# A two-layer decoder step: state-space tables begun at half step four, sums of a Strassen-like product's weights moved, residual loaded in quarters

## The chip, the cores and the metric

The kernel runs on one core of a Trainium2 chip. A core has five engines with a queue each: TensorE for matrix products (PE; its weight loads are listed as PEld), VectorE (DVE), ScalarE (ACT), GpSimd (POOL) and SyncE (SP), which here issues nearly all DMA transfers. The engines work on a shared on-chip memory and wait for each other through semaphores; each takes its own instructions strictly in order. The metric is the time of one execution in microseconds of device time, and the runs are compared by their median. TensorE's clock is granted by the chip at one of two levels, 2.4 GHz (1.00 in the profile's rows) or 1.2 GHz (0.50).

## The reference, cut to what matters

One step of a decoder trunk with two layers, a Conformer convolution layer and a diagonal state-space layer, each followed by a dense SwiGLU network and residual adds. Here 1024 prompt tokens and 64 sample tokens are treated together as 1088 columns; the width is 1024 and the hidden width 2816, in float32.

```python
def swiglu(h, w_gate, w_up, w_down):
    return (jax.nn.silu(h @ w_gate) * (h @ w_up)) @ w_down

for i in range(DEPTH):            # layer 0: convolution, layer 1: state space
    ...
    yp = yp + dp
    yp = yp + swiglu(rms_norm(yp, norm_ffn[i]), w_gate[i], w_up[i], w_down[i])
y_prompt = rms_norm(yp, norm_final)
```

The state-space layer needs tables that depend on its parameters alone (input, output and in-chunk kernel matrices of 64 groups), not on the tokens.

## The kernel before

A float32 product is made of three products of rounded parts: each operand is split into a high part (an ACT copy with rounding) and a low part (a DVE subtraction), and high x high, high x low and low x high are accumulated. `operand` does such a split (L592 on ACT, L593 on DVE), `halfprod` (L600) the matrix products. On top of that the products of the dense network go by a scheme of seven products instead of eight: weights, tokens and outputs are cut into 2 x 2 quarters ("11", "12", "21", "22"), some products take sums or differences of quarters, and the results are added into the outputs' quarters.

The up projection, `ffn_up`, walks over 11 pairs of hidden blocks (`q`), each with a half step for the gate and one for the up weights; a half step is seven products of 24 matmuls. In layer 0, `extra` is called at the end of each half step from the second pair on, with the running number 2q or 2q+1. There it is `tables`, which from number `TU` on begins one of 16 pieces of the state-space tables (`ssm_tables`) per half step and finishes the piece begun the half step before: loads by SP, products on POOL and DVE (L487 to L492, L504 to L506), a copy on ACT (L510), four products on PE into `kr` (L515), eight steps of a sum on DVE (L527, L529), and three stores into DRAM (L476: `st_v`, `st_w`, `st_tt`). Their scratch tiles `b` are in a pool `tab`, eight buffers of one tag.

The down projection, `ffn_down`, works through the products in the order 1, 6, 5, 3, 7, 4, 2, each over 11 hidden pairs `p` and four output blocks `j`. Its token operands were stored by `ffn_up` in DRAM (`td`) and are loaded into `f0b` or `f1b` (L876), its weights into `f0a`, `f1a` (L844), and split into `da` and `db`. Product 6 needs sums of weight quarters, two POOL operations per pair (L856, L857), product 3 one (L863). After a product `collect` (L899) adds the accumulated banks into the residual `xr`, which is loaded as eight whole blocks of 128 x 1088 when the first product is done (L938). The split tokens `db` have three buffers in the pool `bg`. In layer 0 `bg` is opened when the pools `tab` and `mix` of the up projection are closed, at the same address.

The raw weights, tokens and residual blocks share 35 large buffers with the up projection's operands. A scheduler orders each engine's queue by simulating it from the program's order; so the place of an instruction in a queue is not the place in the code.

Of the kernel before, what the change touches and what calls it, by code (L numbers as in the profile page):

```python
# [34 lines left out]
GF = P // C  # L35
GU = GF // 2
NU = G // GU
TU = 5
NLV = 7
EPS = 1e-6  # L40
TB = 68
# [1 line left out]
HT, QT = NT // 2, NT // 4  # L43
NPR, NKP = NFF // 2, NFB // 2
# [18 lines left out]
def decoder_kernel(ctx: ExitStack, tc: tile.TileContext, A):  # L63
    nc = tc.nc
    V, S, PE, GP, SP = nc.vector, nc.scalar, nc.tensor, nc.gpsimd, nc.sync
# [14 lines left out]
    def big(name, dt=F32):  # L80
        return bpool.tile([P, NT], dt, tag="big", name=name)
# [41 lines left out]
    def load_weight(src, name, behind=None):  # L123
        return split_weight(*fetch_weight(src, name), behind)
# [151 lines left out]
    summed = sums.mm  # L276
# [318 lines left out]
    def halfprod(ps, a, ac, an, b, first, last, subs=(0, 1), at=0, more=False):  # L595

        for i, (ah, bh) in enumerate(((0, 0), (0, 1), (1, 0))):
            for s in subs:
                bo = bh * HT + s * QT
                mm = PE.matmul(  # L600
                    ps[s - at][:, :QT],
                    a[:, ah * an + ac : ah * an + ac + P],
                    b[:, bo : bo + QT],
                    start=first and i == 0,
                    stop=last and i == 2,
                    skip_group_check=more,
                )
        return mm

    xd = [[dram.tile([P, NT], F32, name=f"xd{i}_{fb}") for fb in range(NFB)] for i in range(2)]  # L610
# [219 lines left out]

    def ffn_down(layer, name, on_chunk, on_block, before_last, ws, bg, bs):
        order = (1, 6, 5, 3, 7, 4, 2)
        into = {1: "11", 6: "21", 5: "22", 3: "12", 7: "22", 4: "21", 2: "11"}
        NJ = NFB // 2
        kept = {}

        def raw(w, p, use):

            pp = p // 2
            if (w, pp, use) not in kept:  # L840
                t = kept[w, pp, use] = big(f"{name}a{w}_{pp}_{use}")
                m = min(2, NPR - 2 * pp)
                k = ("11", "22", "21", "12").index(w)
                SP.dma_start(  # L844
                    t[:, : m * 512].rearrange("p (t c) -> p t c", t=m),
                    A["down"][layer, k, 2 * pp : 2 * pp + m].rearrange("t p c -> p t c"),
                )
            return kept[w, pp, use][:, (p % 2) * 512 : (p % 2 + 1) * 512]

        def weights(i, p):  # L850

            if i == 1:
                return raw("11", p, 0)
            if i == 6:
                s1, s2 = raw("22", p, 0), raw("21", p, 0)
                GP.tensor_add(s1, s2, s1)  # L856
                GP.tensor_sub(s2, s1, raw("11", p, 0))  # L857
                return s2
            if i == 5:
                return raw("22", p, 0)  # L860
            if i == 3:
                s4 = raw("12", p, 0)
                GP.tensor_sub(s4, s4, raw("21", p, 0))  # L863
                return s4
            if i == 7:
                s3 = raw("21", p, 1)
                GP.tensor_sub(s3, raw("11", p, 1), s3)  # L867
                return s3
            return raw("22" if i == 4 else "12", p, 1)
# [9 lines left out]
        def operands(i, p):  # L879
            last = i == order[-1]  # L880
            if last and p > 2:
                ga = big(f"{name}da{i}_{p}", F32R)
            else:
                ga = wpool.tile([P, D], F32R, tag="wg", name=f"{name}da{i}_{p}", bufs=6)
            if last and p < NPR - 3:
                gb = big(f"{name}db{i}_{p}", F32R)
            else:
                gb = bg.tile([P, NT], F32R, tag="bg", name=f"{name}db{i}_{p}", bufs=3)
            operand(ga, 512, weights(i, p))
            operand(gb, HT, tokens(i, p))  # L890
            return ga, gb

        def quarter(j, w):
            o = (int(w[1]) - 1) * HT
            return xr[2 * j + int(w[0]) - 1][:, o : o + HT]

        def collect(i, j, bank, s):
            c = quarter(j, into[i])[:, s * QT : (s + 1) * QT]
            V.tensor_add(c, c, bank[:, :QT])  # L899
# [6 lines left out]
        def done(j, w, o=None, n=HT):  # L906

            fb = 2 * j + int(w[0]) - 1
            o = (int(w[1]) - 1) * HT if o is None else o
            if on_block is not None:  # L910
                on_block(fb, o, n)
            return fb, o

        xr, early, begun = [], [], {}
        for i in order[:-1]:
            if TAKES[i] is None:
                ps = []
                for j in range(NJ):
                    bank = mm_bank if j < 3 else aux_bank
                    ps.append([bank(f"{name}d{i}_{j}_{s}") for s in range(2)])  # L920
            groups = [(0, 1)] + [(p,) for p in range(2, NPR - 2)] + [(NPR - 2, NPR - 1)]
            for g in groups:
                ops = begun.pop(i) if i in begun else [operands(i, p) for p in g]
                for j in range(NJ):
                    for p, (ga, gb) in zip(g, ops):
                        halfprod(ps[j], ga, j * P, 512, gb, TAKES[i] is None and p == 0, p == NPR - 1, more=TAKES[i] is not None)
                if i == order[-2] and g[0] >= 3:
                    early.append(operands(order[-1], len(early)))
                if i == order[-2] and g[0] == 2:
                    for j in range(NJ):  # L930
                        ss.add(xr[2 * j + 1], 2 * j + 1, HT, HT)
            k = order[order.index(i) + 1]
            if k != order[-1]:
                begun[k] = [operands(k, p) for p in groups[0]]
            if not xr:
                for fb in range(NFB):
                    xr.append(big(f"{name}xr{fb}"))
                    SP.dma_start(xr[fb], xd[layer][fb])  # L938
                xt[:] = xr
            for j in range(NJ):  # L940
                for s in range(2):
                    collect(i, j, ps[j][s], s)
                if i == 4:
                    done(j, "21")
                if i == 7:
                    done(j, "22")
                if i == 3:
                    fb, o = done(j, "12")
                    ss.add(xr[fb], fb, o, HT)
# [6 lines left out]
        i = order[-1]  # L956
# [29 lines left out]
        def end(j, s):  # L986
            collect(i, j, bank[j], s)
            ss.piece = lambda nm: squares[s][:, j * QT : (j + 1) * QT]
            fb, o = done(j, "11", s * QT, QT)
            ss.add(xr[fb], fb, o, QT)  # L990
# [346 lines left out]
    with ExitStack() as st:  # L1337
# [4 lines left out]
        for ci in range(len(CH)):  # L1342
# [11 lines left out]
            for fb in range(ahead):  # L1354
                o, n = CH[ci]
# [4 lines left out]
        for fb in range(ahead, NFB):  # L1360
            t = xt[fb]
            w = load_weight(A["pw2"][fb], f"pw2_{fb}")
# [9 lines left out]
        def tables(f, after):  # L1372

            with tc.issue_after(after.ins), tc.issue_after(loaded.ins):
                for g in begun:
                    next(g, None)
                begun.clear()
                if TU <= f < NU + TU:
                    g = ssm_tables(tab, f - TU)
                    next(g)  # L1380
# [41 lines left out]
    with layer0:  # L1422
        bg, bs = [layer0.enter_context(tc.tile_pool(name=nm, bufs=2)) for nm in ("bg0", "bs0")]
        ffn_down(0, "f0", step_scales, store_x, lambda: [load_stash(fb) for fb in range(2)], ws, bg, bs)
# [251 lines left out]
    with layer1:  # L1676
        bg, fin = [layer1.enter_context(tc.tile_pool(name=nm, bufs=2)) for nm in ("bg1", "bs1")]
        ffn_down(1, "f1", finish, None, None, ws, bg, fin)
# [145 lines left out]
```

## Time and profile before

| | us |
|---|---|
| median of 3 runs | 2283.67 |
| lowest and highest | 2278.57, 2284.53 |
| the profiled execution | 2288.31 |
| its span, first to last instruction | 2286.5 |
| TensorE busy | 2151.0 |
| VectorE busy | 1669.1 |
| GpSimd busy | 1082.2 |

Layer 0's up projection ends and its down projection begins between 954 and 994 us of the span, layer 1's between 2003 and 2024. A timeline row has the start, the duration (of several merged instructions their whole stretch, if there is an xcount), engine, line, operation, output <- inputs, shapes, and in brackets how long the engine was idle before it and what ended that. Rows of SPq are issues of DMA transfers; when the data lands is told by the landing rows.

### The profile page before, as it was taken

Reading aid. Unit: us, or ns where it says so; the run is one execution under the profiler, and the core shown is the slowest. Engines: PE = TensorE matmul, PEld = TensorE weight load, DVE = VectorE, ACT = ScalarE, POOL = GpSimd, SP = SyncE. Lnnn points to the kernel's source line nnn. Section 1 sums busy time; section 2 is a strip of 40 time slices with the busy share of each in tenths; the row PEclk is TensorE's granted clock in tenths of the full one; section 3 lists DMA queues with packets and bytes.
Section 4 is the critical chain, followed back from the end, with each engine's and each line's share of the span. In section 5 each row is a group of like instructions: output and inputs, shape, how many; then the busy total and the mean of one; then the engine's idle time right before and its main releaser. Section 6 shows DMA issues by size and latency. Waiting matters only on the chain. (4 is left out here: it accounts for less than half of the span.)

```text
span 2286.5 us, 39847 instructions
## 1 busy us (share of the span) xinstructions
PE 2151.0 (94%) x15760; PEld 2114.0 (92%) x15760; DVE 1669.1 (73%) x2458; ACT 828.7 (36%) x1618; POOL 1082.2 (47%) x1000
## 2 busy tenths in 40 slices
PE   8998878989999999979998889998999999999997
PEld 7998877989999999979998889998999999998997
DVE  7975867697799999968575973339766666669486
ACT  4201126253333333323453442225333333333363
POOL 3368854465476677635132230116453453428033
PEclk9999988999999999989999999998999999999998
DMA  5489374313244544494295663211322322377532
GB/s 213 158 235 307 127 246 183 131 57 123 92 173 148 189 173 171 158 383 170 94 334 197 232 231 104 92 63 38 124 90 79 117 91 95 121 279 278 186 125 79
DMA packets 198427, 370.73 MB, mean 162 GB/s; under 512 B 15968, under 2 KB 90848, under 8 KB 198240
## 3 DMA queue, kind: packets, MB, share of 16 engines
q1 hardware_dynamic: 173024, 355.34, 44.5%
q10 hardware_dynamic: 25216, 12.85, 2.1%
q8 instruction: 123, 2.02, 0.3%
q14 instruction: 64, 0.52, 0.1%
HBM read 259.34 MB, written 108.79 MB: 161 GB/s over the span
## 5 line engine op out<-in xcount | busy, mean ns | idle before, releaser
L600 PE MATMUL f0d<-f0db,f0da 128*128 128x272 f32 x1848 | 237.0, 290 | 17.5 <-ACT f0db L592 15.6
L600 PEld LDWEIGHTS f0d<-f0db,f0da 128*128 128x128 f32 x1848 | 234.3, 189 | 19.5 <-ACT f0db L592 15.8
L600 PE MATMUL f1d<-f1db,f1da 128*128 128x272 f32 x1848 | 240.7, 292 | 5.3 <-DVE f1da L593 2.2
L600 PEld LDWEIGHTS f1d<-f1db,f1da 128*128 128x128 f32 x1848 | 237.4, 191 | 7.7 <-DVE f1da L593 3.6
L593 DVE TENSOR_TENSOR f0db<-f0b,f0db 128x544 fp32r<-128x544 f32 x77 | 72.7, 950 | 51.7 <-ACT f0db L592 51.6
L593 DVE TENSOR_TENSOR f1db<-f1b,f1db 128x544 fp32r<-128x544 f32 x77 | 74.9, 981 | 45.0 <-ACT f1db L592 44.9
L1095 PE MATMUL dw<-u,tz 128*128 128x128 f32 x640 | 82.2, 291 | 17.8 <-DMA tz<-in_toep 16.6
L1095 PEld LDWEIGHTS dw<-u,tz 128*128 128x128 f32 x640 | 80.0, 206 | 19.3 <-DMA tz<-in_toep 15.4
L592 ACT ACTIVATE f0db<-f0b 128x544 fp32r<-128x544 f32 x77 | 49.9, 656 | 112.8 <-PE f0d L600 91.9
L592 ACT ACTIVATE f1db<-f1b 128x544 fp32r<-128x544 f32 x77 | 50.0, 655 | 98.9 <-PE f1d L600 96.5
L593 DVE TENSOR_TENSOR f0da<-f0a,f0da 128x512 fp32r<-128x512 f32 x77 | 73.0, 954 | 11.9 <-ACT f0da L592 11.6
L593 DVE TENSOR_TENSOR f1da<-f1a,f1da 128x512 fp32r<-128x512 f32 x77 | 75.0, 987 | 6.8 <-ACT f1da L592 6.8
L235 POOL TENSOR_TENSOR f1acc<-f1acc,f1t 128x544 f32<-128x544 f32 x10 | 13.4, 1361 | 111.1 <-ACT f1t L234 111.1
L1634 DVE SCALAR_TENSOR_TENSOR gs<-gv,cst,gs 128x408 f32<-128x408 f32 (+1 forms) x24 | 12.8, 590 | 68.9 <-PE gv L131 68.2
L235 POOL TENSOR_TENSOR f0nacc<-f0nacc,f0nsq 128x544 f32<-128x544 f32 (+1 forms) x13 | 15.5, 1208 | 98.8 <-issue 60.6
L235 POOL TENSOR_TENSOR f1nacc<-f1nacc,f1nsq 128x544 f32<-128x544 f32 (+1 forms) x13 | 16.6, 1284 | 93.6 <-ACT f1nsq L234 93.4
L782 ACT ACTIVATE f0t<-f0t 128x544 f32<-128x544 f32 x44 | 29.1, 661 | 82.0 <-DVE f0t L781 62.8
L782 ACT ACTIVATE f1t<-f1t 128x544 f32<-128x544 f32 x44 | 29.1, 661 | 78.2 <-DVE f1t L781 52.6
L529 DVE SCALAR_TENSOR_TENSOR b<-kr,cst,b 128x448 f32<-128x448 f32 (+6 forms) x112 | 54.5, 487 | 1.2
L592 ACT ACTIVATE f0da<-f0a 128x512 fp32r<-128x512 f32 x77 | 47.2, 620 | 20.4 <-DMA f0a<-in_down 11.0
L592 ACT ACTIVATE f1da<-f1a 128x512 fp32r<-128x512 f32 x77 | 46.9, 622 | 16.2 <-POOL f1a L867 7.3
L491 POOL TENSOR_TENSOR b<-b,b 128x512 f32<-128x512 f32 x32 | 50.5, 1598 | 1.2
(3087 smaller groups left out, 6505.6 us busy)
## 6 DMA issues: line engine op xcount, KB each, us to landing
f0b<-td SPq DMA_DIRECT2D x77, 272.0 KB, 6.7
f1b<-td SPq DMA_DIRECT2D x77, 272.0 KB, 5.3
tz<-in_toep SPq DMA_DIRECT2D x32, 640.0 KB, 6.8
f0a<-in_down SPq DMA_DIRECT2D x40, 512.0 KB, 7.2
f1a<-in_down SPq DMA_DIRECT2D x40, 512.0 KB, 5.7
td<-f0t SPq DMA_DIRECT2D x22, 544.0 KB, 5.8
td<-f1t SPq DMA_DIRECT2D x22, 544.0 KB, 5.2
f0gate<-in_gate SPq DMA_DIRECT2D x22, 512.0 KB, 4.4
```

The source lines that it names most:

```text
L235: self.last = E.tensor_add(acc, acc, t[:, :n])
L491: GP.tensor_mul(v, v, b.unsqueeze(2).to_broadcast([P, GU, 2, PS]))
L529: V.scalar_tensor_tensor(tv[:, :, s:], kv[:, :, : L - s], col(K_MJ, s), tv[:, :, s:], op0=ALU.mult, op1=ALU.add)
L592: S.activation(out[:, :n], x, AF.Copy)
L593: EL.tensor_sub(out[:, n : 2 * n], x, out[:, :n].bitcast(F32))
L600: mm = PE.matmul(ps[s - at][:, :QT], a[:, ah * an + ac : ah * an + ac + P], b[:, bo : bo + QT], start=first and i == 0, stop=last and i == ...
L782: S.activation(c[w], c[w], AF.Silu)
L1095: ln["dw"] = PE.matmul(ps[:, g * P : (g + 1) * P], tz[:, (g % 2) * NM + m].rearrange("p c i -> p (c i)"), uv[:, h * GU + g, PADC - m : PAD ...
L1634: V.scalar_tensor_tensor(sg[:, o : o + n], p[:, :n], col(K_BGV, fb), sg[:, o : o + n], op0=ALU.add, op1=ALU.mult)
```

## The change

Three edits. The tables begin at half step 4 instead of 5. Under product 1 of a down projection, from pair 3 to pair 8, the weight sums of product 6 are made for pairs 0 to 5 (`AHEAD = 3`); a set `summed` keeps them from being made twice. And `fetch` loads quarters of the residual, four of 128 x 544 before the first collect that adds into them, in place of eight whole blocks.

```diff
-TU = 5
+TU = 4
...
     def ffn_down(layer, name, on_chunk, on_block, before_last, ws, bg, bs):
         order = (1, 6, 5, 3, 7, 4, 2)
+        AHEAD = 3
...
-        kept = {}
+        kept, summed = {}, set()
...
             if i == 6:
                 s1, s2 = raw("22", p, 0), raw("21", p, 0)
-                GP.tensor_add(s1, s2, s1)
-                GP.tensor_sub(s2, s1, raw("11", p, 0))
+                if p not in summed:
+                    summed.add(p)
+                    GP.tensor_add(s1, s2, s1)
+                    GP.tensor_sub(s2, s1, raw("11", p, 0))
                 return s2
...
+        here = set()
+
+        def fetch(j, w):
+
+            here.add(w)
+            o = (int(w[1]) - 1) * HT
+            SP.dma_start(quarter(j, w), xd[layer][2 * j + int(w[0]) - 1][:, o : o + HT])
+
...
+                if i == 1 and AHEAD <= g[0] < NPR - 2:
+                    weights(6, g[0] - AHEAD)
...
             if not xr:
                 for fb in range(NFB):
                     xr.append(big(f"{name}xr{fb}"))
-                    SP.dma_start(xr[fb], xd[layer][fb])
                 xt[:] = xr
+            if into[i] not in here:
+                for j in range(NJ):
+                    fetch(j, into[i])
```

What this makes of the queues is seen at two places. The first is the end of layer 0's up projection. On SP, the queue before: `td0_10` are the stores of the last hidden pair, `st_tt7<-b15_8` is the last store of the last table, `f0a` and `f0b` are weights and tokens of the down projection (`f0b1_5` the last tokens of product 1).

```order
L876 DMA f0b1_4_10424<-td0_9_238 128x544
L844 DMA f0a11_5_0_10461<-in_down 128x512
L825 DMA td0_10_239<-f0t10_1_9607 128x1088
L824 DMA td0_10_239<-f0t10_0_9606 128x1088
L827 DMA td0_10_239<-f0u10_9608 128x1088
L829 DMA td0_10_239<-f0t38_9880 128x544
L476 DMA st_tt7_684<-b15_8_10115 128x512
L876 DMA f0b1_5_10465<-td0_10_239 128x544
```

The last table's store stood behind the stores of the last half step; now it stands ahead of the first load of the down projection:

```order
L476 DMA st_w17_676<-b15_7_9880 128x512
L476 DMA st_v17_668<-b15_1_9619 128x512
L476 DMA st_tt7_684<-b14_8_9609 128x512
L1417 DMA ld_w13_12577<-st_w13_672 128x1024
L476 DMA st_tt7_684<-b15_8_9891 128x512
L845 DMA f0a11_0_0_10160<-in_down 128x2x512
L879 DMA f0b1_0_10164<-td0_0_229 128x544
```

It has moved by one half step, in front of the loads and of the stores `td0_10`. On PE at the same place, before, the products `kr15` of the last table stand among those of the last half step `f0up10`:

```order
L600 MATMUL f0up10m1_0_9889<-f0b5_3_4569,f0up10a5_9951 128x272
L600 MATMUL f0up10m1_1_9890<-f0b5_3_4569,f0up10a5_9951 128x272
L515 MATMUL kr15_10107<-b15_5_9875,b15_4_9873 128x128 x3
L600 MATMUL f0up10m7_0_9988<-f0b4_0_4663,f0up10a4_10043 128x272 x2
L600 MATMUL f0up10m7_1_9989<-f0b4_0_4663,f0up10a4_10043 128x272 x2
```

and now between the last two half steps, all four together:

```order
L600 MATMUL f0gate10m1_0_9657<-f0b3_3_4686,f0gate10a3_9848 128x272
L600 MATMUL f0gate10m1_1_9658<-f0b3_3_4686,f0gate10a3_9848 128x272
L515 MATMUL kr15_9883<-b15_5_9634,b15_4_9632 128x128 x4
L600 MATMUL f0up10m1_0_9910<-f0b1_0_3720,f0up10a1_9907 128x272
L600 MATMUL f0up10m1_1_9911<-f0b1_0_3720,f0up10a1_9907 128x272
```

`f0up10` has no table product inside any more.

The second place is the start of layer 1's down projection. On POOL before, the subtraction `f1t38`, which feeds the last store of the last half step, stands ahead of all sums of product 6 (`f1a22`, `f1a21`):

```order
L783 TENSOR_TENSOR f1t10_0_20275<-f1t10_0_20275,f1r_15597 128x544
L828 TENSOR_TENSOR f1t38_20508<-f1t10_1_20276,f1u10_20277 128x544
L856 TENSOR_TENSOR f1a22_0_0_21117<-f1a21_0_0_21119,f1a22_0_0_21117 128x512 x2
L857 TENSOR_TENSOR f1a21_0_0_21119<-f1a22_0_0_21117,f1a11_0_0_20758 128x512 x2
L856 TENSOR_TENSOR f1a22_1_0_21212<-f1a21_1_0_21214,f1a22_1_0_21212 128x512 x2
L857 TENSOR_TENSOR f1a21_1_0_21214<-f1a22_1_0_21212,f1a11_1_0_20823 128x512 x2
```

and now behind six of them:

```order
L783 TENSOR_TENSOR f1t10_0_20283<-f1t10_0_20283,f1r_15605 128x544
L859 TENSOR_TENSOR f1a22_0_0_20894<-f1a21_0_0_20896,f1a22_0_0_20894 128x512 x2
L860 TENSOR_TENSOR f1a21_0_0_20896<-f1a22_0_0_20894,f1a11_0_0_20766 128x512 x2
L859 TENSOR_TENSOR f1a22_1_0_20967<-f1a21_1_0_20969,f1a22_1_0_20967 128x512 x2
L828 TENSOR_TENSOR f1t38_20516<-f1t10_1_20284,f1u10_20285 128x544
L860 TENSOR_TENSOR f1a21_1_0_20969<-f1a22_1_0_20967,f1a11_1_0_20831 128x512 x2
```

The six sums of the first pairs passed the subtraction; layer 0 has the same order there. On SP at that place, before, eight residual blocks stand between the first weights of product 6 and the next:

```order
L844 DMA f1a21_0_0_21119<-in_down 128x2x512
L876 DMA f1b6_0_21125<-td1_0_240 128x544
L876 DMA f1b6_0_21125<-td1_1_241 128x544
L938 DMA f1xr0_21138<-xd1_0_221 128x1088
L938 DMA f1xr1_21140<-xd1_1_222 128x1088
L938 DMA f1xr2_21142<-xd1_2_223 128x1088
L938 DMA f1xr3_21144<-xd1_3_224 128x1088
L938 DMA f1xr4_21146<-xd1_4_225 128x1088
L938 DMA f1xr5_21148<-xd1_5_226 128x1088
L938 DMA f1xr6_21150<-xd1_6_227 128x1088
L938 DMA f1xr7_21152<-xd1_7_228 128x1088
L844 DMA f1a22_1_0_21212<-in_down 128x2x512
```

and now four quarters, with the weights of pairs 6 and 7 close behind:

```order
L879 DMA f1b6_0_21151<-td1_0_240 128x544
L879 DMA f1b6_0_21151<-td1_1_241 128x544
L906 DMA f1xr0_21162<-xd1_0_221 128x544
L906 DMA f1xr2_21164<-xd1_2_223 128x544
L906 DMA f1xr4_21166<-xd1_4_225 128x544
L906 DMA f1xr6_21168<-xd1_6_227 128x544
L879 DMA f1b6_1_21234<-td1_2_242 128x544
L879 DMA f1b6_1_21234<-td1_3_243 128x544
L879 DMA f1b6_2_21297<-td1_4_244 128x544
L879 DMA f1b6_2_21297<-td1_5_245 128x544
L845 DMA f1a22_3_0_21358<-in_down 128x2x512
L845 DMA f1a21_3_0_21360<-in_down 128x2x512
```

The loads of the weights of pairs 0 to 5 have gone up among those of product 1, and the other residual quarters follow later in the queue.

## Rows read from the trace of the kernel before

**Rows 1.** The page's first part: busy time, share, count of instructions.

```profile
PE 2151.0 (94%) x15760; PEld 2114.0 (92%) x15760; DVE 1669.1 (73%) x2458; ACT 828.7 (36%) x1618; POOL 1082.2 (47%) x1000
```

**Rows 2.** PE's waits: total us, times, longest.

```profile
PE f0d L600 <- ACT f0db L592: 15.6, 1, 15.6
```

**Rows 3.** Timeline of PE, layer 0: last half steps, start of the down projection.

```profile
926.87 3.39 PE L600 MATMUL f0up9m<-f0b,f0up9a 128*128 128x272 f32 x24 [0.84 <-DVE f0t L760]
...
953.03 1.05 PE L515 MATMUL kr<-b,b 128*128 128x128 f32 x8
953.84 15.49 PE L600 MATMUL f0up10m<-f0b,f0up10a 128*128 128x272 f32 x120
...
971.43 6.33 PE L600 MATMUL f0up10m<-f0b,f0up10a 128*128 128x272 f32 x48 [1.43 <-ACT f0t L754]
977.60 0.38 PE L515 MATMUL kr<-b,b 128*128 128x128 f32 x2
993.59 41.30 PE L600 MATMUL f0d<-f0db,f0da 128*128 128x272 f32 x314 [15.61 <-ACT f0db L592]
```

**Rows 4.** Timeline of ACT at the same place.

```profile
992.88 1.75 ACT L592 ACTIVATE f0db<-f0b 128x544 fp32r<-128x544 f32 x3 [11.15 <-issue]
```

**Rows 5.** Timeline of SP at the same place: issues of transfers.

```profile
970.23 0.92 SPq L876 DMA_DIRECT2D f0b<-td  x2
...
987.98 0.32 SPq L829 DMA_DIRECT2D td<-f0t  x1
988.76 0.48 SPq L476 DMA_DIRECT2D st_tt<-b  x1
```

**Rows 6.** Tile f0b between 969 and 972: issue to landing.

```profile
DMA to landing us min/median/max: 3.8/5.2/6.2
```

**Rows 7.** Tile st_tt between 985 and 1000: issue to landing.

```profile
DMA to landing us min/median/max: 3.8/3.8/3.8
```

**Rows 8.** Windows: length, busy PE, PEld, DVE, ACT, POOL, clock, DMA share, GB/s.

```profile
982.00:993.50 11.50, 0.00 (x0) 0.00 (x0) 6.59 (x13) 0.62 (x2) 1.33 (x1) 0.50 0.99 356
993.50:998.00 4.50, 4.41 (x22) 4.42 (x23) 2.00 (x3) 1.13 (x3) 0.95 (x1) 0.58 1.03 397
```

**Rows 9.** Windows in layer 1: product 1, product 6, and behind it.

```profile
2024.40:2057.60 33.20, 33.20 (x267) 33.20 (x266) 19.47 (x29) 11.71 (x21) 11.62 (x9) 1.00 0.91 348
2057.60:2099.05 41.45, 36.91 (x261) 35.60 (x261) 40.67 (x27) 15.51 (x27) 41.45 (x25) 0.92 0.82 298
...
2100.00:2110.00 10.00, 10.00 (x71) 10.00 (x70) 8.50 (x12) 2.37 (x4) 4.52 (x3) 0.84 0.73 263
```

**Rows 10.** Timeline of DVE, layer 1: token splits without and with POOL beside.

```profile
2036.85 0.73 DVE L593 TENSOR_TENSOR f1db<-f1b,f1db 128x544 fp32r<-128x544 f32 x1 [1.69 <-ACT f1db L592]
...
2066.01 3.55 DVE L593 TENSOR_TENSOR f1db<-f1b,f1db 128x544 fp32r<-128x544 f32 x2
```

**Rows 11.** Timeline of POOL, layer 1: sums without and with DVE beside.

```profile
2053.58 2.54 POOL L856 TENSOR_TENSOR f1a<-f1a,f1a 128x512 f32<-128x512 f32 x2 [9.57 <-DMA f1a<-in_down]
...
2065.50 3.47 POOL L856 TENSOR_TENSOR f1a<-f1a,f1a 128x512 f32<-128x512 f32 x2
```

**Rows 12.** Timeline of PE, layer 1, start of the third product.

```profile
2099.05 4.30 PE L600 MATMUL f1d<-f1db,f1da 128*128 128x272 f32 x19 [1.74 <-DVE f1xr L899]
```

**Rows 13.** Chain of work: start, duration; one undisturbed half step.

```profile
1644.27 21.10 PE f1gate2m L600 x168
```

**Rows 14.** Timeline of DVE in the last half step of layer 0.

```profile
961.51 1.59 DVE L505 TENSOR_TENSOR b<-bc,Ai 128x576 f32<-128x576 f32 x1
...
968.67 1.16 DVE L529 SCALAR_TENSOR_TENSOR b<-kr,cst,b 128x192 f32<-128x192 f32 x3
```

**Rows 15.** Timeline of SP, layer 1: the residual's loads.

```profile
2033.47 5.88 SPq L938 DMA_DIRECT2D f1xr<-xd  x8
```

## The prediction

> **What bounds the kernel now.** I read the engine shares first: the matmul engine (PE) is busy for 94% of the span and VectorE (DVE) for 73% [rows 1], so a change can only pay where PE stands or runs slowly. The view of waits names the longest single one: the first matmul of layer 0's down projection waits 15.6 us for ACT's high part of its token operand, `f0db` [rows 2]. The timelines of that place tell whose wait it is. The last half step of the up projection, `f0up10`, starts at 953.84, stalls once for 1.43, ends about 978, and the down projection starts at 993.59 [rows 3]. ACT writes `f0db` at 992.88 after 11.15 us of idleness that no instruction on another engine ended [rows 4]. The tokens it reads had been issued at 970.23 [rows 5] and such loads land within 6.2 us [rows 6], so they were there by 978. What came at the right moment is the store of the last state-space table, issued at 988.76 [rows 5] and landed 3.8 us later [rows 7], at 992.6. The pool that holds `f0db` is opened after the table pool is closed and takes its memory: the down projection stood until the last table had left. While PE stood, the granted clock fell to 0.50, the 1.2 GHz level, and it was 0.58 on average in the first 4.5 us of the next work [rows 8].
>
> The second place is layer 1's second down product (number 6). Its predecessor runs at full rate, 267 matmuls in 33.2 us; product 6 takes 41.45 us for 261, with DVE busy for 40.67 and POOL for all of it [rows 9]. A DVE operand split costs 0.73 alone and 3.55/2 = 1.78 beside POOL; a POOL sum costs 2.54/2 = 1.27 alone and 3.47/2 = 1.74 beside DVE [rows 10, 11]. So a POOL sum delays a busy DVE by about 1.05 us. PE then waits for DVE in small pieces, the last of 1.74 for the residual add [rows 12].
>
> **The change part by part.** A matmul at full rate takes 21.10/168 = 0.1256 us [rows 13], and a down product has 2 x 3 x 4 x 11 = 264 of them, 33.2 us.
>
> *Tables one half step earlier.* All 16 tables keep their loads, stores, four matmul products and DVE, ACT and POOL work; the order shows them at the same places of a half step, one half step sooner, on all five queues. The cost moves with them: up to the start of `f0up10` there is one more set of kernel products (953.03 to 953.84, 0.81) and one more stalled half step, of which the typical large stall is 0.84 [rows 3]. I charge both: `f0up10` would start at 953.84 + 0.81 + 0.84 = 955.5. It has no table products inside, and of DVE's table work only the last eight-step sum; the three operations that build the next table (the longest 1.59 [rows 14]) are gone, and so are POOL's that slowed DVE. So I cost its 1.43 stall at zero; it ends at 955.5 + 21.1 = 976.6. Is the last table out by then? In the trace the table sum that began with the products at 953.03 had its last steps at 968.67 to 969.8 [rows 3, 14]. With up to 3 x 1.59 = 4.8 us less in front and 1.7 later in start, I put its end at 967 (estimate), and the first tokens, issued behind that store on SP, at 968 + 5.2 = 973 [rows 6], high part and matmul by 975. Ends: 0 if all of it hides, 3 if that DVE work is no shorter than now (tokens 970.23 + 1.7 + 6.2 = 978.1, and ACT's split). I take 1. Gain: 993.59 - 976.6 = 17.0, less 1. Clock: 22 matmuls ran in the 4.5 us of [rows 8], where 36 fit: 14 x 0.1256 = 1.7 gained. With PE not idle the clock has no cause to fall there.
>
> *Sums of product 6 under product 1, residual by quarters.* Twelve of 22 sums, with six loads of 512 KB, move ahead on SP past the last loads of product 1 and the stores of the last half step, and on POOL six sums stand in front of the subtraction that feeds the last of these stores. SP's queue holds the tokens of product 1's end behind that store. In layer 0 those sums wait for about 5.2 MB of loads (at 397 GB/s [rows 8] 13 us, so until about 980), run till about 988, and the store follows at 989, hardly later than the 987.98 of now [rows 5]; its tokens land by 1002 and are read at 976.6 + 10 x 3.0 = 1007. That is 5 us of cover, and each us beyond would be PE idle. The residual is loaded as 16 transfers instead of 8 per layer; eight more issues of SP lie in its idle time. Eight whole blocks, 4.46 MB at 397 GB/s or 11 us, stand now between the first weights of product 6 and the rest [rows 15]; then it is a quarter of that, 2.8 us. No PE wait ends in these loads, so the bytes gain nothing by themselves; with four weight loads less in line they bring the other ten sums some 13 us earlier, most of them under product 1.
>
> What that is worth in layer 1: product 6 lost 41.45 - 261 x 0.1256 = 8.7, and the clock behind it 1.1 more (71 matmuls in 10 us where 79.6 fit [rows 9]). With only the 11 sums for product 3 beside it, DVE needs 22 x 0.73 + 11 x 1.05 + 3 for the collects = 31 of 33.2 us: no stall. With 21 sums it needs 41 and the 8.7 stay. By the earlier loads it is nearer the first; I leave 1.5 of a possible 0 to 8.7. Product 6 of layer 0 I leave as it is.
>
> What the sums cost where they go: DVE is busy for 19.47 of product 1's 33.2 us, with 9 POOL operations beside it [rows 9]. If all 22 sums ran there, 14 more x 1.05 gives 34.2, 1.0 too much; in layer 0 the tail of `f0up10` adds five splits and sums, 3.6 us, so 4.6. If they spread, nothing. DVE's lead is up to three token buffers, 9 us. I take 2 for layer 0, where they all come late, of 0 to 4.6, and nothing more for layer 1.
>
> The Trainium skill (SBUF — State Buffer, Who interferes with whom) speaks against this part: a DVE operation with two SBUF inputs and a POOL operation that reads SBUF exclude each other for a whole instruction. By that, a sum would hold DVE for 1.27 instead of the 1.05 of the rows, and 22 sums would cost product 1 some 5 us more per layer where there is no slack. The measured pair, 1.78 and 1.74 against 0.73 and 1.27 [rows 10, 11], is a little better than exclusion of the whole, so I sum by the rows.
>
> Sum: 17.0 + 1.7 + 8.7 + 1.1 = 28.5, less 1 + 2 + 1.5 = 24.0. The profiled execution took 2288.31 (span 2286.5) and would take 2264.3; it stands 4.6 over the median of 2283.67, and I carry the difference to that: 2259.7.
>
> **The rivals.** *The POOL price moves instead of going.* Under product 1 DVE begins with no lead, since the tail of the up projection is on it too; if the sums start as that tail runs, each layer's first product loses what layer 1's product 6 loses now, 8.7 + 1.1. Gain 28.5 - 1 - 19.6 = 7.9, time 2275.8. For it: the 25 POOL operations and 40.67 us of DVE in [rows 9]. Against: 12 sums, not 25, stand there for certain. The skill's exclusion (same page) is this rival's mechanism, at its higher price.
>
> *The wait at the transition stays*, because not the table store but something else held the pool's memory (ACT's wait in the order covers several semaphores). Then only layer 1 gains, 8.7 + 1.1 - 1.5 = 8.3: 2275.4. Against: the landing fits to within 0.3 us.
>
> *Slower: tables in an earlier half step stall more.* The tables would meet the SP loads or the DVE work of gate and up steps in the other parity, and each of 16 half steps would cost 1.5 us more to eat the gain and 1.9 more to end slower by 0.3%; at 2.5 it is 40 - 24, so 2299.7. Against: stalls there are 0.84 and less now, and the pieces sit in the same places of the half step as before.
>
> **How the numbers follow.** Forecast 0.68, around 2259.7, from 2271.5 (28.5 - 3 - 4.6 - 8.7 = 12.2 gained) to 2255.2 (28.5). First rival 0.13, second 0.08, slower one 0.04, a gain beyond 28.5 0.04, mixtures 0.03. The shown runs spread from 2278.57 to 2284.53, so I reach 3 below the full gain, 2252, and above to 2277, which takes in both rivals on the faster side. A measurement of this kernel can tell about 0.3%, 6.9 us: faster than 2276.8 is the forecast and nearly all of two rivals, 0.90; within, 0.06; slower, 0.04.
>
> **What would show it.** Right: no PE gap above 2 us between `f0up10` and the down projection and a granted clock of 1.00 there; ACT's `f0db` by about 976 on the scale of the trace before; the sums of pairs 0 to 5 before the middle of product 1; product 6 of layer 1 within 35 us; the residual add no longer waited for. Wrong: a token load of product 1's end that PE waits for in layer 0, DVE full under product 1 with PE waiting in pieces of half a us, the granted clock at 0.5 there, or longer half steps with tables.

## The result, and the profile after

The changed kernel takes 2262.31 us in the median of 4 runs (2257.37 to 2262.85), the kernel before 2284.1 beside it: 0.9901 of the time, 95% interval 0.9882 to 0.9919, or 18 to 27 us less. A second group of runs gave 0.9886 (0.9865 to 0.9907). The profiled execution took 2261.8, its span 2260.0.

I cut the span into stretches with clear ends. A runs from the start of `f0up1` to that of `f0up10`, B from there to the last matmul of layer 0's down projection, C to the start of `f1up10`, D to the last matmul of layer 1's down projection. Before `f0up1` and behind D the change touches nothing.

| us | up to f0up1 | A | B | C | D |
|---|---|---|---|---|---|
| before | 542.5 | 411.4 | 280.3 | 768.7 | 268.4 |
| after | 543.2 | 416.2 | 263.0 | 764.5 | 257.8 |
| after, a second execution | 540.1 | 416.2 | 261.8 | 760.4 | 257.8 |

A, B and D together lose 23.0 us (24.1 in the second execution; differences taken before rounding). C differs by 4.1 between two executions of the same program, so its 4.2 against before can't be put down to the change.

The matmul engine's share of the span rose from the 94% of [rows 1] to 95%. This is the first part of the page of after:

```profile
PE 2146.2 (95%) x15760; PEld 2110.1 (93%) x15760; DVE 1662.1 (74%) x2458; ACT 827.2 (37%) x1618; POOL 1081.7 (48%) x1000
```

PE's timeline of after at layer 0's transition answers [rows 3] (start, duration, instructions, idle time before and what ended it):

```profile
976.11 3.27 PE L600 MATMUL f0up10m<-f0b,f0up10a 128*128 128x272 f32 x24 [1.28 <-ACT f0t L754]
979.22 0.67 PE L600 MATMUL f0d<-f0db,f0da 128*128 128x272 f32 x4
979.73 3.17 PE L600 MATMUL f0up10m<-f0b,f0up10a 128*128 128x272 f32 x24
982.74 8.95 PE L600 MATMUL f0d<-f0db,f0da 128*128 128x272 f32 x70
993.58 116.66 PE L600 MATMUL f0d<-f0db,f0da 128*128 128x272 f32 x912 [1.89 <-DVE f0db L593]
```

The wait of 15.61 is gone: the down projection follows the last product of `f0up10` without a gap, 11 us earlier than the 993.59 of [rows 3]. The stall of 1.28 inside `f0up10` stayed, and 11 us later a new one of 1.89 stands. The timelines of DVE and, below it, of POOL at that place name its cause:

```profile
988.71 1.81 DVE L822 TENSOR_TENSOR f0u<-f0t 128x544 f32<-128x544 f32 x1
992.18 0.71 DVE L826 TENSOR_TENSOR f0u<-f0t,f0u 128x544 f32<-128x544 f32 x1
992.82 2.50 DVE L593 TENSOR_TENSOR f0db<-f0b,f0db 128x544 fp32r<-128x544 f32 x2
```

```profile
988.41 3.27 POOL L859 TENSOR_TENSOR f0a<-f0a,f0a 128x512 f32<-128x512 f32 x2 [0.17 <-DMA f0a<-in_down]
992.97 1.76 POOL L828 TENSOR_TENSOR f0t<-f0t,f0u 128x544 f32<-128x544 f32 x1 [1.30 <-DVE f0u L826]
```

The early sums (L859, L860) run beside the last operations of the up projection on DVE. One of these takes 0.71 alone and 1.81 beside a sum, and the token split that PE needs stands behind them.

The stretches of after (PE, PEld, DVE, ACT, POOL, then granted clock) are two of layer 0's product 1, then layer 1's products 1 and 6, which answer [rows 9]:

```profile
982.20:994.50 12.30, 10.41 (x83) 10.18 (x82) 12.12 (x9) 4.86 (x9) 10.84 (x7) 1.00 1.05 394
994.50:1015.40 20.90, 20.90 (x156) 20.90 (x156) 17.57 (x16) 7.61 (x13) 12.08 (x9) 0.92 0.97 361
2008.40:2041.60 33.20, 33.20 (x266) 33.20 (x266) 29.86 (x32) 12.87 (x23) 23.35 (x14) 1.00 0.93 348
2041.60:2075.00 33.40, 33.40 (x268) 33.40 (x267) 28.10 (x32) 13.12 (x24) 20.74 (x15) 1.00 0.86 306
```

In layer 1 product 6 runs at full rate, 268 matmuls in 33.4 us where 261 took 41.45: POOL has 15 operations there instead of 25, DVE is busy for 28 us instead of 41. The residual add of [rows 12] is no longer waited for. In layer 0 DVE is full (12.12 of 12.30) just where the 1.89 arises.

Stretch A grew. These are the windows of the first two half steps with tables, first of before (its third row is a later up half step) and then of after:

```profile
626.86:648.84 21.98, 21.98 (x178) 21.98 (x177) 20.77 (x29) 8.23 (x18) 15.54 (x11) 1.00 0.38 133
648.84:671.28 22.44, 22.35 (x178) 22.08 (x177) 21.28 (x32) 8.43 (x18) 15.23 (x11) 1.00 0.62 220
671.28:695.30 24.02, 22.93 (x178) 22.23 (x177) 22.80 (x31) 8.04 (x19) 17.50 (x13) 1.00 0.36 124
```

```profile
606.49:629.91 23.42, 22.84 (x179) 22.20 (x177) 21.46 (x30) 8.34 (x18) 15.45 (x11) 1.00 0.56 208
629.91:653.88 23.97, 22.90 (x178) 22.23 (x177) 22.76 (x31) 7.99 (x18) 17.46 (x13) 1.00 0.36 124
```

A half step with a table needs 21.10 + 0.81 = 21.91 of matmuls. Before, the first two lost 0.6 together; after, where they fall on a gate and then an up half step, they lose 3.6. Later ones repeat in both kernels like these of after:

```profile
794.77 1.05 PE L515 MATMUL kr<-b,b 128*128 128x128 f32 x8
...
814.48 3.39 PE L600 MATMUL f0gate7m<-f0b,f0gate7a 128*128 128x272 f32 x24 [0.58 <-DVE f0t L760]
817.71 1.05 PE L515 MATMUL kr<-b,b 128*128 128x128 f32 x8
...
831.20 6.46 PE L600 MATMUL f0up7m<-f0b,f0up7a 128*128 128x272 f32 x48 [0.23 <-ACT f0u L754]
838.49 3.38 PE L600 MATMUL f0up7m<-f0b,f0up7a 128*128 128x272 f32 x24 [0.83 <-DVE f0t L760]
841.71 1.05 PE L515 MATMUL kr<-b,b 128*128 128x128 f32 x8
```

From `kr` to `kr` the gate half step takes 22.94 and the up half step 24.00: they lose 1.0 and 2.1 us, about twice the idle times in brackets (0.58; 0.23 and 0.83). In these rows the bracket starts about 0.4 us after the next matmul would have been due: 48 matmuls at 0.1256 are 6.03, the row says 6.46.

### The profile page after: what moved, and what is told of

Same layout as the page of the kernel before. It is cut to its first block, busy times and chain, and to the rows that moved or that the text cites. A ratio compares the mean times of both kernels' runs of the same rounds, so it can differ in the third digit from the quotient of the medians.

```text
span 2260.0 us, 39851 instructions
## 1 busy us (share of the span) xinstructions
PE 2146.2 (95%) x15760; PEld 2110.1 (93%) x15760; DVE 1662.1 (74%) x2458; ACT 827.2 (37%) x1618; POOL 1081.7 (48%) x1000
## 4 chain that ended last, share of the span: by engine, by line
PE 62%; DVE 21%; DMA 5%; issue 4%; POOL 3%; ACT 2%; ACTq 1%; SPq 1%; DVEq 0%; POOLq 0%
PE f1d L600 9%; PE f0d L600 9%; PE gg L131 4%; PE gv L131 4%; PE p L131 4%; PE pv L131 3%; PE pg L131 2%; PE dw L1110 1%; DVE b L529 1%; DVE f0t L786 1%; ACTq L459 1%; DVE f0t L781 1%; PE f1gate10m L600 1%; PE f1up9m L600 1%; PE f1gate9m L600 1%
## 5 line engine op out<-in xcount | busy, mean ns | idle before, releaser
L600 PE MATMUL f1d<-f1db,f1da 128*128 128x272 f32 x1848 | 234.6, 288 | 0.8 <-DVE f1db L593 0.4
L600 PEld LDWEIGHTS f1d<-f1db,f1da 128*128 128x128 f32 x1848 | 232.7, 188 | 1.8 <-DVE f1db L593 1.0
L529 DVE SCALAR_TENSOR_TENSOR b<-kr,cst,b 128x448 f32<-128x448 f32 (+6 forms) x112 | 54.4, 486 | 1.2
```

Of the source, the lines that this page charges most:

```text
L529: V.scalar_tensor_tensor(tv[:, :, s:], kv[:, :, : L - s], col(K_MJ, s), tv[:, :, s:], op0=ALU.mult, op1=ALU.add)
L600: mm = PE.matmul(ps[s - at][:, :QT], a[:, ah * an + ac : ah * an + ac + P], b[:, bo : bo + QT], start=first and i == 0, stop=last and i == ...
```

## The experiments

Each kernel was compared with runs of the kernel before on its own chip. The last column sums A, B and D of its trace against before.

| kernel | ratio, 95% interval | A | B | D | A+B+D, us |
|---|---|---|---|---|---|
| tables only | 0.9969, 0.9955 to 0.9983 | 416.1 | 266.8 | 268.4 | -8.7 |
| sums only | 0.9971, 0.9956 to 0.9986 | 412.4 | 285.7 | 260.4 | -1.5 |
| quarters only | 0.9930, 0.9908 to 0.9952 | 411.4 | 278.1 | 258.8 | -11.7 |
| sums and quarters | 0.9977, 0.9961 to 0.9994 | 412.4 | 283.3 | 257.7 | -6.6 |
| tables and quarters | 0.9885, 0.9865 to 0.9905 | 416.3 | 261.1 | 259.0 | -23.6 |
| tables and sums | 0.9929, 0.9903 to 0.9954 | 416.2 | 269.9 | 258.6 | -15.3 |
| after, again | 0.9886, 0.9865 to 0.9907 | 416.2 | 261.8 | 257.8 | -24.1 |
| sums later | 0.9898, 0.9877 to 0.9920 | 416.1 | 259.7 | 261.5 | -22.7 |
| tokens apart | 0.9994, 0.9981 to 1.0008 | 411.4 | 276.2 | 268.4 | -3.9 |
| tokens apart, quarters | 0.9891, 0.9868 to 0.9913 | 412.4 | 266.4 | 259.0 | -22.2 |
| first step on ACT | 0.9874, 0.9852 to 0.9896 | 410.2 | 261.3 | 257.8 | -30.7 |
| quarters, ACT in gate half steps | 0.9884, 0.9862 to 0.9907 | 413.8 | 261.4 | 259.1 | -25.8 |

### Each part by itself

**Tables only** (the kernel before with one edit).

```diff
-TU = 5
+TU = 4
```

> Only the tables are begun one half step sooner; sums and residual are as before. Theory: the wait at the start of layer 0's down projection goes here and nowhere else. The trace of after has that start 11.4 us earlier (993.59 to 982.2), and with the 1.7 of clock behind it this kernel gains 13 us, to about 2271, with layer 1's product 6 still at 41.5 us and its residual add still waited for. The 4.2 us that after gains between the two layers' down projections should show here in part or not at all if they belong to the sums, and whole if they come from the stage's start being moved: 2267 then. Rival (the gain at the transition is lost in product 6 of layer 0, whose 22 sums no longer have the standing time of PE to be loaded in): 2275 to 2279.

The wait at the transition is gone as in after, yet the gain is half of the theory's 13 us; the rival was right. Windows of layer 0's product 1 and of most of its product 6 in this kernel's trace, then PE's rows in product 6:

```profile
982.80:1016.00 33.20, 33.20 (x267) 33.20 (x266) 18.79 (x31) 11.82 (x21) 8.34 (x7) 1.00 0.99 380
1016.00:1049.50 33.50, 30.67 (x235) 29.55 (x235) 32.56 (x21) 13.32 (x23) 33.50 (x20) 1.00 0.97 357
```

```profile
1036.61 8.04 PE L600 MATMUL f0d<-f0db,f0da 128*128 128x272 f32 x62 [0.76 <-DVE f0da L593]
1057.46 42.74 PE L600 MATMUL f0d<-f0db,f0da 128*128 128x272 f32 x337 [2.96 <-DVE f0xr L899]
```

The third product begins at 1057.46, 41.5 us behind product 6's start, with DVE and POOL full and the residual add waited for: [rows 9, 12] of layer 1 over again. In the kernel before, the time in which PE stood had let these sums get ahead: 13 POOL operations lay under product 1, where there are 7 here, and product 6 lost about 2.6 us (247 matmuls in 33.60, where 267 fit) instead of 8. These are its windows of layer 0's products 1 and 6:

```profile
993.50:1027.00 33.50, 33.41 (x253) 33.42 (x254) 21.76 (x21) 11.66 (x21) 19.46 (x13) 0.94 1.04 399
1027.00:1060.60 33.60, 32.29 (x247) 30.97 (x247) 32.28 (x31) 12.89 (x22) 28.86 (x19) 1.00 0.71 250
```

**Quarters only** (`fetch` and the four calls before a collect, with `TU = 5` and no early sums).

> Only the residual is loaded by quarters; tables and sums as before. Theory (the weights behind the residual come 8 us sooner, and the POOL sums of product 6 with them, but all 22 sums still stand under product 6 with 11 for product 3 behind them): product 6 of layer 1 loses about half of its 8.7 us, 36 to 39 us instead of 41.5, the kernel gains 3 to 6, 2278 to 2281. Rival (the number of sums under product 6 decides and not when its loads land): 41 us and 2284.

The theory's direction was right and its half was far too little: D falls by 9.5 of the 10.6 that the whole change gains there. The first fence is SP's queue (the residual's first quarters, then the weights of product 6), the second layer 1's product 6, both of this kernel:

```profile
2022.00 2.36 SPq L906 DMA_DIRECT2D f1xr<-xd  x4
2024.92 1.73 SPq L845 DMA_DIRECT2D f1a<-in_down  x2
```

```profile
2045.90:2079.10 33.20, 32.90 (x259) 32.31 (x258) 32.15 (x27) 12.31 (x22) 30.24 (x19) 1.00 1.00 379
```

The weights are issued 3 us after the residual's first transfer, where eight whole blocks, issued from 2033.47 on [rows 15], kept them back for 7, until 2040.38. That brings 13 instead of 9 POOL operations under product 1, and 19 instead of 25 are left for product 6, which runs at full rate, though DVE has 32.15 of 33.2 us to do.

**Sums only** (twelve sums ahead, residual whole, `TU = 5`) and **sums and quarters** (the changed kernel with `TU = 5`).

```diff
+                if i == 1 and AHEAD <= g[0] < NPR - 2:
+                    weights(6, g[0] - AHEAD)
```

> Only twelve of the 22 sums stand ahead under product 1; tables at half step five, residual in whole blocks. Theory (by the prediction's sum the ten late sums and the eleven of product 3 still meet in product 6, 21 of 25): product 6 of layer 1 stays at 38 to 41 us and the kernel gains 0 to 4, 2280 to 2284. Rival (the number of sums that are gone from product 6 decides): about 34 us, the kernel at 2274 to 2276.

> Sums ahead and residual by quarters, but the tables at half step five as before. Theory: the first matmul of layer 0's down projection still waits 15 us or more for f0db, the granted clock falls there, and only layer 1 gains: product 6 in 33 to 34 us instead of 41.5, with the clock 10.6 in all, to about 2273.5. Rival (the tokens' reordering on SP or the free bandwidth shorten the wait too): the wait is under 10 us and the time under 2268. If the 4.2 us between the layers belong to this part: 2269.

In layer 1 the sums alone do most of the work (D 260.4; the rival was right on product 6), and with the quarters D falls by the 10.6 that the theory had. But neither theory saw that the wait at the transition would grow. From the traces of sums and quarters (SP, ACT, PE, and DVE beside the sums):

```profile
991.63 0.32 SPq L476 DMA_DIRECT2D st_tt<-b  x1
998.38 1.75 ACT L592 ACTIVATE f0db<-f0b 128x544 fp32r<-128x544 f32 x3 [16.85 <-DMA td<-f0t]
999.08 7.11 PE L600 MATMUL f0d<-f0db,f0da 128*128 128x272 f32 x44 [22.73 <-ACT f0db L592]
```

```profile
979.16 1.79 DVE L786 TENSOR_TENSOR f0t<-f0t,f0u 128x544 f32<-128x544 f32 x1
980.88 0.67 DVE L529 SCALAR_TENSOR_TENSOR b<-kr,cst,b 128x448 f32<-128x448 f32 x1
```

The sums slow DVE's operations in front of the last table's sum: the store is issued 4.4 us later behind `f0up10`'s start than in the kernel before. It is issued at 991.63 and lands 6.6 us later, at 998.2, instead of 3.8, and `f0db` is written at 998.38. The longer landing can't be put down to the sums: without them it took 6.1 in tokens apart, below. (The row of ACT names a store `td` that SP issued 0.4 us later, at 992.05. That kind of store was not what `f0db` waited for: in after it is issued at 994.76, 18 us behind the first `f0db`.) So the early sums need the tables out of the way.

### Two parts together

**Tables and quarters** (the changed kernel without the two lines of the early sums) and **tables and sums** (with the residual in whole blocks).

> The changed kernel without its early sums: tables at half step four, residual by quarters, all 22 sums of product 6 begun behind product 1 as before. Three stretches are compared: A from the start of f0up1 to that of f0up10 (before 411.4, after 416.2), B from there to the last matmul of layer 0's down projection (280.3, 263.0), D from the start of f1up10 to the last matmul of layer 1's down projection (268.4, 257.8). Theory (the tables alone gave A +4.7 and B -13.5, the quarters alone B -2.2 and D -9.5, and the sums add nothing to them): A 416, B 264 to 265, D 259, and a time within 4 us of that of after. Rival (in layer 0 the sums are needed, since product 6 there loses what the standing time of PE used to hide): B 267 or more, D 259, some 5 us or more slower than after.

> The changed kernel with the residual in eight whole blocks again: tables at half step four and early sums stay. Theory (with the tables out of the way the early sums do not lengthen the wait at the transition as they did with the tables at half step five, 22.7 instead of 15.6; in layer 1 the sums alone gave D 260.4): A 416, B 263 to 266, D 260 to 261, within 5 us of after. Rival (the early sums hold POOL and DVE back at the transition here too): B 270 or more.

Without the early sums the kernel is as fast as with them: 0.9885 against 0.9901 and 0.9886, and A+B+D -23.6 against -23.0 and -24.1. Its product 6 of layer 0 runs at nearly full rate:

```profile
1012.90:1046.10 33.20, 32.76 (x257) 32.09 (x256) 32.85 (x24) 12.13 (x21) 30.34 (x19) 1.00 1.04 399
```

Sums and tables without the quarters stop at 0.9929. There B is 269.9, the rival's value: besides the 1.89, PE waits 4.37 for the residual add behind product 6 in layer 0. DVE is busy all through that wait: operand splits, which take 1.74 to 1.79 each beside POOL's sums for product 3, stand ahead of the add.

**After, again**, and **sums later** (`AHEAD = 6`, so six sums are ahead).

> The changed kernel once more, unaltered, beside the others of this group. A 416, B 263, D 258 as before, with the 1.9 us wait of f0d for DVE's f0db about 14 us after the down projection's start; 20 to 26 us faster than before. If the sums of product 6 are worth something under product 1, it is faster than the kernel without them, which was 26.6 faster; if they cost there (theory: B 263.0 with them, 261.1 without), it is some 2 us slower than that.

> The changed kernel with the early sums begun three pairs later (six of product 6's 22 sums under product 1, behind pair 6, instead of twelve behind pair 3). Theory (the 1.9 us wait in layer 0 comes from sums on POOL beside DVE's last operations of the up projection, each slowed from 0.72 to 1.8 us, in the 12 us after the transition): with the sums later the wait and the half clock behind it are gone, B 261 to 262 instead of 263.0, A and D as in after, 1 to 3 us faster than after. Rival (the wait is for the token loads, which the sums' weight loads push back on SP): it stays or moves, B 263 or more.

With the sums later, DVE's last operations of the up projection are done before POOL begins, and the 1.89 is gone:

```profile
987.39 0.72 DVE L822 TENSOR_TENSOR f0u<-f0t 128x544 f32<-128x544 f32 x1
988.78 0.72 DVE L826 TENSOR_TENSOR f0u<-f0t,f0u 128x544 f32<-128x544 f32 x1
991.26 3.26 POOL L859 TENSOR_TENSOR f0a<-f0a,f0a 128x512 f32<-128x512 f32 x2 [0.32 <-DMA f0a<-in_down]
```

B falls to 259.7, somewhat more than the theory's 261 to 262. But in layer 1 seventeen POOL operations now crowd product 1, PE waits there for 1.34, and D rises to 261.5: no gain in all.

### The cause of the wait at the transition

**Tokens apart** (the kernel before, with five token operands out of the table pool's memory), and the same **with quarters**.

```diff
-            if last and p < NPR - 3:
+            if last and p < NPR - 3 or layer == 0 and i == 1 and p < 5:
                 gb = big(f"{name}db{i}_{p}", F32R)
```

> The kernel before, tables at half step five, with the token operands of the first five pairs of layer 0's product 1 in the pool of big tiles instead of bg0, whose memory was the table pool's. Theory (the first matmul waited for that memory to come free, which it did when the last table's store had landed): ACT writes the first f0db as soon as its tokens have landed, at 978 to 980 on the scale of before; the first f0d matmul starts at 979 to 982 instead of 993.6, 25 to 28 us behind f0up10's start instead of 39.8; B is 266 to 270 instead of 280.3 (the last table's sum is then on DVE beside the first operands, 2 or 3 us of small waits); 10 to 14 us faster than before, with A and D as before. Rival (the loads or their queue, not the memory, held the first operand): the first f0d still comes 38 us or more behind f0up10's start, and the time is that of before.

> Tables at half step five, no early sums, the first five pairs' tokens in memory of their own, and the residual by quarters. Theory (with the memory apart the wait at the transition went, 25.1 us from f0up10's start to f0d's instead of 39.8, but the time that PE stood had hidden the 22 sums of product 6, which then held product 6 of layer 0 up as they do in layer 1; loading the residual by quarters frees both): A 411, f0d 25 us behind f0up10, product 6 of layer 0 in 33 to 35 us, B 266 to 270 instead of 276.2, D 259; 18 to 23 us faster than before, though neither the memory apart (1.3) nor the quarters (14.7, of which 2 in B) gave that alone. Rival (product 6's loss in layer 0 comes from the last table's work on DVE, not from the residual's place in the queue): B 274 or more, 12 to 15 us faster.

PE and ACT of tokens apart:

```profile
979.68 0.66 ACT L592 ACTIVATE f0db<-f0b 128x544 fp32r<-128x544 f32 x1 [1.94 <-DMA f0b<-td]
984.86 15.32 PE L600 MATMUL f0d<-f0db,f0da 128*128 128x272 f32 x120
...
1065.29 77.49 PE L600 MATMUL f0d<-f0db,f0da 128*128 128x272 f32 x604 [4.49 <-DVE f0xr L899]
```

```profile
1020.00:1065.00 45.00, 37.42 (x285) 35.87 (x284) 42.11 (x30) 16.59 (x28) 42.69 (x26) 1.00 0.89 325
```

The operand is written as soon as its tokens land, and the products start 25.1 us behind `f0up10`'s start (959.73) instead of 39.8. So it was the memory. What freed it shows on the sixth pair, whose operand still lies there: its `f0db` is written at 1002.06, and the last table's store, issued at 995.89, lands 6.1 us later, at 1002.0. PE waits 2.60 for it. With quarters ACT's row even names the store:

```profile
1005.35 1.76 ACT L592 ACTIVATE f0db<-f0b 128x544 fp32r<-128x544 f32 x3 [0.38 <-DMA st_tt<-b]
```

But tokens apart is no faster than before (0.9994): product 6 loses what the wait had hidden. With the quarters added it reaches 0.9891, with the tables where they were. The gains of the two parts alone, 1.4 and 16 us by their ratios, do not add up to these 25; B falls by 9.8 more.

### What half steps with tables wait for

**First step on ACT** (the changed kernel), and **quarters, ACT in gate half steps** (without the early sums, and on ACT only for tables with `half == 0`).

```diff
-        V.tensor_scalar(tv, kv, col(K_MJ, 0), None, op0=ALU.mult)
+        S.activation(tv, kv, AF.Copy, scale=col(K_MJ, 0))
```

> The changed kernel with the first of the eight steps of each table sum (a scaling of the kernel's bank, 0.74 us on DVE) on ACT, which is busy for a third of these half steps. Theory (in the half steps with tables DVE is the bound: busy for 21.8 of 22.9 and 22.8 of 24.0 us, where the matmuls need 21.9): each of some 15 half steps becomes 0.6 to 0.8 us shorter, 22.3 and 23.3; A falls from 416.2 to 405 to 408, and the kernel gains 8 to 11 us on after. Rival (the stalls come from the latency of a chain, PE's bank to ACT and DVE and back, and not from DVE's sum of work): the half steps stay at 22.9 and 24.0 or grow, A is 415 to 420.

> Tables at half step four, residual by quarters, no early sums, and the first step of a table's sum on ACT where its bank is filled in a gate half step (there that took the stall away, 22.94 to 21.99 us), on DVE where it is filled in an up half step (there it cost 0.2 more on ACT, 24.03 to 24.23, with a new stall for ACT). Theory (DVE bounds the gate half steps, ACT's place in the chain the up ones): gate half steps 22.0, up half steps 24.0, A 408 to 410 instead of 416.2, B 261, D 259, 32 to 35 us faster than before, the best so far. Rival (what is gained in the gate half step is given back in the up half step behind it, whose start is DVE's lead): up half steps of 24.5 or more, A 412 to 414, and 28 to 30.

PE of the first kernel, then of the second:

```profile
797.58 1.05 PE L515 MATMUL kr<-b,b 128*128 128x128 f32 x8
819.57 1.05 PE L515 MATMUL kr<-b,b 128*128 128x128 f32 x8
827.10 6.44 PE L600 MATMUL f0up7m<-f0b,f0up7a 128*128 128x272 f32 x48 [0.45 <-ACT f0t L754]
843.83 1.05 PE L515 MATMUL kr<-b,b 128*128 128x128 f32 x8
```

```profile
815.80 1.05 PE L515 MATMUL kr<-b,b 128*128 128x128 f32 x8
823.57 6.46 PE L603 MATMUL f0up7m<-f0b,f0up7a 128*128 128x272 f32 x48 [0.68 <-ACT f0t L757]
840.79 1.05 PE L515 MATMUL kr<-b,b 128*128 128x128 f32 x8
```

0.74 us less on DVE takes the loss of a gate half step away (21.99), but the up half step behind it grows to 24.26, and to 24.99 where only the gate half steps are relieved: the rival of the last run, DVE's work handed on to the next half step. A falls by 6.0, short of the 8 to 11 of the theory, and by 2.4. In the median these two took 2256.7 and 2259.7 us; the intervals of both overlap those of after, so no version here is shown to beat it.

## Why the prediction was right, step by step

Forecast 24.0 us, measured 21.8 by the medians. Sign, size and both places were right, but not each term.

- **The transition's cause** was right: with the memory apart, or with the last table's store earlier, the wait is gone, and an operand left in that memory was written when the store had landed. ACT's `f0db` came at 976.24, as told (976), but `f0up10` had begun 3 us later than told, on the scale of before, so a match that close is in part luck.
- **The term of 17.0 was mis-sized.** The step that failed is "one more stalled half step, of which the typical large stall is 0.84". A grew by 4.8, where the sum had 0.81 + 0.84 = 1.65. The one more half step lost 1.0, near the 0.84. The other 3.0 fall on the first two half steps with tables (3.6 against 0.6), for which the sum had nothing: "The cost moves with them" took all pieces to cost the same in the other parity. I had read the idle time of one row; the pitch from `kr` to `kr` would have shown in the trace of before that a gate half step loses 1.0 and an up half step 2.1, and that the first two got off with 0.6. There the first half step with tables is an up one with 29 DVE operations of 20.77 us; a later one has 31 of 22.80, and the first up half step of after 31 of 22.76. That this is why it was cheap is argued from the rows and not tested. The start of `f0up10` came 5.5 later, 0.7 of that from the work in front of A.
- **The stall of 1.43 in `f0up10`, costed at zero, stayed** (1.28), though the three operations for a next table are gone; with the rest of the table's sum on DVE it is ended by ACT as before. Together with the last step this makes the down projection begin some 11 us earlier, not 16.
- **The late tokens, 1, cost nothing**: they were there before `f0up10` had ended. The last store of product 1's tokens was issued at 994.76 instead of the 989 of the prediction, but no wait of PE ended in those tokens either.
- **The clock, 1.7**: at the transition it stayed at 1.00. But behind the 1.89 it fell again, and 156 matmuls ran in 20.9 us where 166 fit, 1.3 us; so 1.9 + 1.3 = 3.2 stands for the 2 that I had taken for the early sums in layer 0, within the 0 to 4.6. In the second execution it was 1.9 and a further wait of 0.66, at full clock.
- **"Product 6 of layer 0 I leave as it is"** came true for the whole change, but without a reason. Tables only and tokens apart show that the removed wait had been its cover, and that about 8 us would have been lost there. The quarters pay for that, a gain in layer 0 that the sum doesn't have.
- **Layer 1, 8.7 + 1.1 - 1.5 = 8.3** became 10.6 of D: nothing of the 8.7 stayed. That the earlier loads bring the sums forward was the right mechanism. The quarters do it alone (9.5); the twelve moved sums, for which the text argued at length, add 1 where the quarters are, and take as much in layer 0 (B is 0.7 to 1.9 longer with them).
- **The first rival**, the POOL price under product 1, was real in layer 0 at a third of its size there (3.2 of 8.7 + 1.1), and came to nothing in layer 1, where DVE was busy for 29.86 of 33.2 without a wait. The two others did not come about; longer half steps with tables did, though by 4.0 in all, not 40.

A and B, the transition among them, gave 3.2 us less than forecast, D 2.3 more: part of the agreement is two errors that cancel.

On the price of DVE beside POOL, the rows of after and of sums and quarters repeat [rows 10, 11]: 0.72 becomes 1.79 to 1.81, with sums of 1.74. The Trainium skill (SBUF — State Buffer, Who interferes with whom) says that a DVE instruction with at most one SBUF input, outside the two-port modes, does not contend with POOL. The trace agrees: L529, which reads the PSUM bank `kr`, a column of scalars and one SBUF tile, takes 0.67 at 980.88 in sums and quarters, with POOL busy beside it and 1.79 for the operation in front. In the kernel before, with POOL idle, the same step takes as long:

```profile
983.44 0.68 DVE L529 SCALAR_TENSOR_TENSOR b<-kr,cst,b 128x448 f32<-128x448 f32 x1
```

## What to carry to other kernels

Before a wait is removed, look for the work that catches up while the engine stands: here the weight sums of the next product had their cover from it, and removing the wait alone was worth 0 to 7 us of 15. Price a repeated stall by the pitch between equal events, not by the idle time in brackets, and look at the half steps where a pattern begins, which need not cost what the later ones do. A bulk transfer that is needed late should not stand in a queue ahead of loads that are needed early: that one reordering gave most of the gain in layer 1 and freed layer 0's product as well.

## What was not expected of the hardware

The same 1.9 us wait of PE in layer 0 was followed by a lower clock in one execution of the same program and not in the other. These are the windows of after and of its second execution, 10 us from the start of that wait:

```profile
991.69:1001.69 10.00, 8.11 (x52) 8.11 (x53) 10.00 (x8) 2.64 (x5) 8.72 (x6) 0.83 0.93 352
988.90:998.90 10.00, 7.45 (x58) 7.23 (x58) 10.00 (x8) 3.33 (x6) 8.71 (x6) 1.00 0.90 341
```

With the clock at 0.83 of full on average, 52 matmuls ran; at 1.00 it was 58, although a second wait, of 0.66, falls into that window. Two more executions had the wait: in tables and sums (1.89) the clock fell to 0.83 as well, with first step on ACT (2.01) it stayed at 1.00. So the length of the wait alone does not tell; what does is not shown here. The 6 matmuls are 0.75 of the 1.2 us by which B of the two executions differs.
